# First rows of the first phase in a written order: ada_w ahead of x, three of eight row blocks on TensorE, the modulation on ScalarE

## The chip, the cores and the metric

One core of a Trainium2 chip runs the whole program in one launch. TensorE (PE) multiplies, VectorE (DVE), ScalarE (ACT) and GpSimd (POOL) do elementwise work, SyncE (SP) issues the large loads. The metric is the device time of one execution in microseconds (us), lower is better.

## The reference

Two layers of a decoder trunk on x of 256 tokens by 1024, in fp32. A layer has three sub-layers, each modulated by a conditioning vector c: a half-step SwiGLU (d_ff 2816), a token mixer (gated DeltaNet, MoBA attention and mLSTM heads side by side, one projection in, one out), and another SwiGLU. The change touches the head of the first sub-layer of layer 0:

```
mod = (silu(c) @ ada_w[l] + ada_b[l]).reshape(b, 3, 3, 1024)
h   = x * (1 + scale) + shift                  # mod[:, 0, 1], mod[:, 0, 0]
a, b = split(h @ w13, 2)                       # w13: 1024 x 5632
y   = (silu(a) * b) @ w2
x   = layer_norm(ALPHA*x + 0.5*(1 + gate)*y, ln_g, ln_b)
```

## The kernel before

An fp32 product is made of three products of rounded parts: `split` (lines 94 to 102) rounds a weight tile to `hi` on ScalarE (L98) and takes `lo` as the rest on VectorE (L100); `mm3` (L104 to L106) accumulates hi by xh, hi by xl and lo by xh in PSUM.

The first phase (layer 0, first SwiGLU) begins with `first_rows`. It computes the first seven of 22 column blocks of w13 while the modulation is still being made, k block by k block (the 1024 rows of w13 in eight blocks of 128). For each k, `modulate(k)` loads a piece of ada_w, `araw` (1024 rows by 128 shift and 128 scale columns, 1 MB in two DMAs), and a row block of w13, `raw` (two DMAs of 448 KB). VectorE sums the eight 128-row blocks of the piece, each times its column of silu(c), into `ada` (L594, L596); TensorE sums `ada` over its partitions with a matmul of one column (L598); VectorE adds the bias columns `abc` (L600, L601), ScalarE makes xh (L603), VectorE xm and xl (L605, L606). Then come 42 products of 256 columns: seven blocks f, two halves ab, three each. x itself is loaded first, in one DMA (L1299), and transposed into xT (L567). The seven PSUM banks (`pss`: four named pg, three pacc) are opened with a product by zero (L580).

`param_columns` (L186 to L195) transposes four groups of parameter rows into columns on TensorE (L183), with a copy on VectorE (L184): abc for both layers, lnc (layer norm), cvc (convolutions).

Behind the first rows, `ffn` handles the other column blocks in chunks of two, their raw tiles loaded 1 MB at a time (L82), with `sg` (silu, L631), `h` (L633), `hh` and `hl` (L638, L639) per block. In between stand background pieces for later modulations: `adacc` on VectorE (L253, L255), with their own 1 MB pieces of ada_w.

Except for SyncE, whose order is the program's, a scheduler decides the order of each engine's instructions from its own estimate, over the whole program. Buffers set the rest: `araw` has three, `raw` four, `hi` eight, `lo` four.

The mixer (one per layer) holds, for the steps below: `at` (L935, VectorE; a product of the DeltaNet heads with its decay), `MB` (L1175, VectorE, and L1176, ScalarE; mLSTM gate terms that arrive by a DMA through DRAM), and `U` (L1053, ScalarE; a copy of the DeltaNet heads' solved values out of PSUM).

## Time and profile before

| | us |
|---|---|
| median of 3 runs | 1238.44 (1237.76, 1238.44, 1243.74) |
| the profiled execution itself | 1244.06 |
| its span | 1242.3 |
| mean granted TensorE clock | 0.966 of full |

The profile shows one execution. Starts are us from the span's start. A row of a timeline gives start, duration, engine, line, operation, output and inputs, the number of instructions in the row, and in brackets the idle time ahead of it and what ended that. Rows with several instructions are runs without a gap; an instruction's duration overlaps the next one's start. TensorE's ends are modelled, so the distance from start to start is the better measure there. The granted clock is 1.00 at 2.4 GHz and 0.50 at 1.2 GHz. An fp32 matmul leaves two records.

### The profile page before, as it was taken

The numbers are of one execution on the slowest core, as the hardware profiler recorded it, in microseconds if no ns is written. First come the engines' busy times: TensorE is split into PE (matmuls) and PEld (weight loads), VectorE is DVE, ScalarE is ACT, GpSimd is POOL, SyncE is SP. The second block draws the span as 40 slices with busy tenths as digits, with TensorE's granted clock in tenths as the row PEclk, the third lists the DMA queues.
The fourth block names the chain that finished last, engine by engine and source line by source line (L and its number), as shares of the span: only waits on it lengthen the run. The fifth ranks groups of instructions, "written<-read, shape, count | busy, mean of one in ns | idle before, by whom it ended". The sixth has DMA issues, their size and how long they took to land.

```text
span 1242.3 us, 21704 instructions
## 1 busy us (share of the span) xinstructions
PE 1169.5 (94%) x8896; PEld 1075.6 (87%) x8896; DVE 899.2 (72%) x1451; ACT 577.9 (47%) x946; POOL 104.0 (8%) x174
## 2 busy tenths in 40 slices
...
GB/s 306 343 306 369 283 410 277 117 178 130 120 174 57 35 269 373 338 275 303 261 11 345 333 282 260 254 239 77 186 129 97 170 46 74 256 220 181 244 203 34
DMA packets 171523, 266.02 MB, mean 214 GB/s; under 512 B 5406, under 2 KB 136986, under 8 KB 171424
## 3 DMA queue, kind: packets, MB, share of 16 engines
...
q14 instruction: 30, 0.25, 0.1%
HBM read 263.56 MB, written 1.06 MB: 213 GB/s over the span
## 4 chain that ended last, share of the span: by engine, by line
PE 74%; DVE 9%; DMA 6%; ACT 5%; issue 3%; POOL 2%; SPq 0%; DVEq 0%; ACTq 0%; POOLq 0%
PE pg L105 14%; PE pg L106 14%; PE pg L104 14%; PE pacc L106 7%; PE pacc L105 7%; PE pacc L104 7%; DMA raw<-in_ffn_w_dram 4%; DVE lo L100 2%; ACT hi L98 2%; PE pg L220 1%; POOL xt L961 1%; DMA raw<-in_w_in_dram 1%; PE pg L228 1%; POOL X L963 1%; ACT xh L446 1%
## 5 line engine op out<-in xcount | busy, mean ns | idle before, releaser
L100 DVE TENSOR_TENSOR lo<-raw,hi 128x1024 fp32r<-128x1024 f32 (+3 forms) x332 | 395.1, 1196 | 146.7 <-PE pg L105 69.5
L98 ACT ACTIVATE hi<-raw 128x1024 fp32r<-128x1024 f32 (+4 forms) x352 | 352.3, 1027 | 305.7 <-DMA raw<-in_ffn_w_dram 144.6
L104 PE MATMUL pg<-xh,hi 128*128 128x256 f32 x1568 | 448.2, 288 | 5.7 <-ACT xh L603 2.9
L105 PE MATMUL pg<-xl,hi 128*128 128x256 f32 x1568 | 448.6, 286 | 1.5 <-DVE xl L606 1.5
L106 PE MATMUL pg<-xh,lo 128*128 128x256 f32 x1568 | 448.3, 286 | 0.2 <-DVE lo L100 0.2
L104 PEld LDWEIGHTS pg<-xh,hi 128*128 128x128 f32 x1568 | 302.8, 194 | 8.5 <-ACT xh L603 3.8
L105 PEld LDWEIGHTS pg<-xl,hi 128*128 128x128 f32 x1568 | 305.0, 194 | 3.2 <-DVE xl L606 2.0
L106 PEld LDWEIGHTS pg<-xh,lo 128*128 128x128 f32 x1568 | 304.7, 195 | 0.8 <-DVE lo L100 0.4
L255 DVE SCALAR_TENSOR_TENSOR adacc<-araw,sc__132,adacc 128x1024 f32<-128x1024 f32 x118 | 151.1, 1281 | 8.6 <-DMA araw<-in_ada_w_dram 8.0
L105 PE MATMUL pacc<-lo,hh 128*128 128x512 f32 (+1 forms) x352 | 128.9, 367 | 2.4 <-DVE lo L100 2.4
L104 PE MATMUL pacc<-hi,hh 128*128 128x512 f32 (+1 forms) x352 | 130.4, 371 | 0.0
L106 PE MATMUL pacc<-hi,hl 128*128 128x512 f32 (+1 forms) x352 | 129.6, 369 | 0.0
L172 POOL TENSOR_TENSOR lsm<-lsm,mhalf 128x1 f32<-128x1 f32 x12 | 7.5, 627 | 888.6 <-DVE lsm L344 888.6
L105 PEld LDWEIGHTS pacc<-lo,hh 128*128 128x128 f32 x352 | 66.5, 189 | 16.8 <-DVE lo L100 3.6
L104 PEld LDWEIGHTS pacc<-hi,hh 128*128 128x128 f32 x352 | 66.2, 188 | 12.8 <-issue 0.7
L106 PEld LDWEIGHTS pacc<-hi,hl 128*128 128x128 f32 x352 | 66.0, 188 | 11.8
L631 ACT ACTIVATE sg<-pg 128x256 f32<-128x256 f32 x79 | 29.4, 373 | 65.9 <-PE pg L106 65.8
L104 PE MATMUL pacc<-hi,xh 128*128 128x512 f32 (+1 forms) x80 | 38.1, 476 | 20.7 <-ACT xh L446 20.7
L638 ACT ACTIVATE hh<-h 128x256 fp32r<-128x256 f32 x82 | 33.7, 411 | 41.4 <-DVE h L633 41.3
L639 DVE TENSOR_TENSOR hl<-h,hh 128x256 fp32r<-128x256 f32 x82 | 34.5, 421 | 22.5 <-ACT hh L638 22.5
L722 DVE SCALAR_TENSOR_TENSOR cy<-pg,cvc,cy 128x255 f32<-128x255 f32 (+2 forms) x90 | 40.0, 474 | 7.0 <-ACT cy L720 6.7
L104 PEld LDWEIGHTS pacc<-hi,xh 128*128 128x128 f32 x80 | 19.3, 241 | 27.5 <-ACT xh L446 25.8
...
## 6 DMA issues: line engine op xcount, KB each, us to landing
...
```

Source lines behind the costliest of these rows:

```text
L98: nc.scalar.activation(hi, v, AF.Copy)
L100: nc.vector.tensor_tensor(lo, v, hi.bitcast(F32), op=ALU.subtract)
L104: nc.tensor.matmul(o, ah, bh, start=first, stop=False)
L105: nc.tensor.matmul(o, ah, bl, start=False, stop=False)
L106: nc.tensor.matmul(o, al, bh, start=False, stop=last)
L220: nc.tensor.matmul(pt[:, m:m + 1], acc[:, m * 128:(m + 1) * 128], ones[:, 0:1], start=True, stop=True)
L228: nc.tensor.matmul(pts[h], ones, acc[:, h * 512:(h + 1) * 512], start=True, stop=True)
L255: nc.vector.scalar_tensor_tensor(acc, raw[:, kk, :], sc_[:, k:k + 1], acc, op0=ALU.mult, op1=ALU.add)
L631: nc.scalar.activation(sg, pa, AF.Silu)
L638: nc.scalar.activation(hh[:, f, :], h, AF.Copy)
L639: nc.vector.tensor_sub(hl[:, f, :], h, hh[:, f, :].bitcast(F32))
L722: nc.vector.scalar_tensor_tensor(y[:, s:], ps[:, :T - s], w(3 - s), y[:, s:], op0=ALU.mult, op1=ALU.add)
```

## The change

`first_rows` is written anew, its instructions on TensorE, VectorE and ScalarE in the order of the code (`manual_schedule`), and not by the scheduler.

- Loads: the first ada_w piece goes ahead of x, x comes in two halves of 512 columns with the first w13 block in between, and the loads run two k ahead.
- Modulation: VectorE sums five of the eight row blocks. TensorE takes the other three from the raw piece, with a column of silu(c) as moving operand (L610), and adds VectorE's sum (L611): for each k, eight fp32 matmuls of one column where there were two.
- ScalarE makes xm as well as xh, and all four copies of xT.
- The last two PSUM banks serve for the transposes of x first and are opened later.
- `param_columns` transposes only the first group up front; the other three (`more_columns`) are issued behind the first rows.

The diff, with the code that comes in:

```diff
--- before.py
+++ after.py
@@ -191,8 +191,8 @@
             nc.scalar.dma_start(rows[48:96, 2, :], ln_b.rearrange("l s (k p) -> (l s k) p", p=128))
             nc.scalar.dma_start(rows[0:72, 3, :], gdn_conv.rearrange("l j (k p) -> (l j k) p", p=128))
             nc.scalar.dma_start(rows[72:120, 3, :], mlstm_conv.rearrange("l j (k p) -> (l j k) p", p=128))
-            for i, (n, dst) in enumerate(((72, abc[:, 0:72]), (72, abc[:, 72:144]), (96, lnc), (120, cvc))):
-                column(rows[:n, i, :], n, dst)
+            column(rows[:72, 0, :], 72, abc[:, 0:72])
+            return lambda: [column(rows[:n, i, :], n, dst) for i, n, dst in ((1, 72, abc[:, 72:144]), (2, 96, lnc), (3, 120, cvc))]
 
         rc = ap_.tile([KD, 128], F32, tag="gate", name="rc", bufs=2)
         nc.sync.dma_start(rc, c.rearrange("o (k p) -> (o k) p", p=128))
@@ -560,60 +560,120 @@
 
             xin = state["xa"]
             xT = ap_.tile([128, KD, T], F32, tag="n", name="xT")
-            for q in range(0, KD, 2):
-                pt = ps_g()
+            xh = ap_.tile([128, KD, T], F32R, tag="xh", name="xh")
+            xl = ap_.tile([128, KD, T], F32R, tag="xl", name="xl")
+            cps = ps_acc(1)
+            pss = [ps_g() for _ in range(4)] + [ps_acc(t) for t in (0, 0, 1)][:nf - 4]
+            raws, wrs, xms = {}, {}, {}
+
+            nv = 5
+
+            def load_mod(k):
+                raws[k] = fpool[0].tile([128, KD, 2, 128], F32, tag="araw", name="araw", bufs=3)
+                for j in range(2):
+                    o = j * D + k * 128
+                    nc.sync.dma_start(raws[k][:, :, j, :], ada_w[0, :, o:o + 128].rearrange("(k p) f -> p k f", p=128))
+
+            def load_w(k):
+                wrs[k] = wp.tile([128, 2, nf * 128], F32, tag="raw", name="raw", bufs=4)
+                for ab in range(2):
+                    nc.sync.dma_start(wrs[k][:, ab, :], w13[l, i, k * 128:(k + 1) * 128, ab * DFF:ab * DFF + nf * 128])
+
+            def load_x(q):
+                sl = slice(q * 512, (q + 1) * 512)
+                nc.sync.dma_start(xin[:, :, sl], x[0].rearrange("(t p) d -> p t d", p=128)[:, :, sl])
+
+            def turn(q):
+
+                pt = pss[(0, 1, nf - 2, nf - 1)[q // 2]]
                 for k in (q, q + 1):
                     for t in range(2):
                         nc.tensor.transpose(pt[:, (k - q) * 256 + t * 128:(k - q) * 256 + (t + 1) * 128],
                                             xin[:, t, k * 128:(k + 1) * 128], ident)
-                v = pt.rearrange("p (a b) -> p a b", a=2)
-                if q % 4:
-                    nc.vector.tensor_copy(xT[:, q:q + 2, :], v)
-                else:
-                    nc.scalar.activation(xT[:, q:q + 2, :], v, AF.Copy)
-            xh = ap_.tile([128, KD, T], F32R, tag="xh", name="xh")
-            xl = ap_.tile([128, KD, T], F32R, tag="xl", name="xl")
-            cps = ps_acc(1)
-            pss = [ps_g() for _ in range(4)] + [ps_acc(t) for t in (0, 0, 1)][:nf - 4]
-
-            for ps in pss:
+                nc.scalar.activation(xT[:, q:q + 2, :], pt.rearrange("p (a b) -> p a b", a=2), AF.Copy)
+
+            def open_(ps):
+
                 nc.tensor.matmul(ps, zero.to_broadcast([1, 128]), zero.to_broadcast([1, 512]), start=True, stop=False)
-            wrs = {}
 
             def modulate(k):
-                raw = fpool[0].tile([128, KD, 2, 128], F32, tag="araw", name="araw", bufs=3)
-                for j in range(2):
-                    o = j * D + k * 128
-                    nc.sync.dma_start(raw[:, :, j, :], ada_w[0, :, o:o + 128].rearrange("(k p) f -> p k f", p=128))
-                wrs[k] = wp.tile([128, 2, nf * 128], F32, tag="raw", name="raw", bufs=4)
-                for ab in range(2):
-                    nc.sync.dma_start(wrs[k][:, ab, :], w13[l, i, k * 128:(k + 1) * 128, ab * DFF:ab * DFF + nf * 128])
+                raw = raws[k]
                 a = fpool[0].tile([128, 2, 128], F32, tag="h", name="ada", bufs=2)
-                for kk in range(KD):
+                for kk in range(nv):
                     if kk == 0:
                         nc.vector.tensor_scalar(a, raw[:, kk], sc_[:, kk:kk + 1], None, op0=ALU.mult)
                     else:
                         nc.vector.scalar_tensor_tensor(a, raw[:, kk], sc_[:, kk:kk + 1], a, op0=ALU.mult, op1=ALU.add)
                 for j in range(2):
-                    nc.tensor.matmul(cps[:, 2 * k + j:2 * k + j + 1], a[:, j, :], ones[:, 0:1], start=True, stop=True)
+                    o = cps[:, 2 * k + j:2 * k + j + 1]
+                    for kk in range(nv, KD):
+                        nc.tensor.matmul(o, raw[:, kk, j, :], sc_[:, kk:kk + 1], start=kk == nv, stop=False)
+                    nc.tensor.matmul(o, a[:, j, :], ones[:, 0:1], start=False, stop=True)
+
+            def apply(k):
                 sh, sc1 = modc[0][:, k:k + 1], modc[0][:, 8 + k:9 + k]
-                nc.vector.tensor_add(sh, cps[:, 2 * k:2 * k + 1], abc[:, k:k + 1])
                 nc.vector.scalar_tensor_tensor(sc1, cps[:, 2 * k + 1:2 * k + 2], 1.0, abc[:, 8 + k:9 + k],
                                                op0=ALU.add, op1=ALU.add)
+                nc.vector.tensor_add(sh, cps[:, 2 * k:2 * k + 1], abc[:, k:k + 1])
                 nc.scalar.activation(xh[:, k, :], xT[:, k, :], AF.Identity, bias=sh, scale=sc1)
-                xm = fpool[0].tile([128, T], F32, tag="sg", name="xm", bufs=2)
-                nc.vector.tensor_scalar(xm, xT[:, k, :], sc1, sh, op0=ALU.mult, op1=ALU.add)
-                nc.vector.tensor_sub(xl[:, k, :], xm, xh[:, k, :].bitcast(F32))
-
-            modulate(0)
-            for k in range(KD):
-                if k + 1 < KD:
-                    modulate(k + 1)
+                xms[k] = fpool[0].tile([128, T], F32, tag="sg", name="xm", bufs=2)
+                nc.scalar.activation(xms[k], xT[:, k, :], AF.Identity, bias=sh, scale=sc1)
+
+            def high(k):
+                ws = []
                 for ab in range(2):
-                    hi, lo = split(wrs[k][:, ab:ab + 1, :])
-                    for f in range(nf):
-                        mm3(pss[f][:, ab * 256:(ab + 1) * 256], hi[:, 0, f * 128:(f + 1) * 128],
-                            lo[:, 0, f * 128:(f + 1) * 128], xh[:, k, :], xl[:, k, :], False, ab == 1 and k == KD - 1)
+                    hi = wp.tile([128, 1024], F32R, tag="hi", name="hi", bufs=8)[:, :nf * 128]
+                    nc.scalar.activation(hi, wrs[k][:, ab, :], AF.Copy)
+                    ws.append((hi, wp.tile([128, 1024], F32R, tag="lo", name="lo", bufs=4)[:, :nf * 128]))
+                return ws
+
+            def low(k, ab, w):
+                nc.vector.tensor_tensor(w[ab][1], wrs[k][:, ab, :], w[ab][0].bitcast(F32), op=ALU.subtract)
+
+            def low_x(k):
+                nc.vector.tensor_sub(xl[:, k, :], xms[k], xh[:, k, :].bitcast(F32))
+
+            def products(k, ab, w, f0=0, f1=nf):
+                hi, lo = w
+                for f in range(f0, f1):
+                    mm3(pss[f][:, ab * 256:(ab + 1) * 256], hi[:, f * 128:(f + 1) * 128],
+                        lo[:, f * 128:(f + 1) * 128], xh[:, k, :], xl[:, k, :], False, ab == 1 and k == KD - 1)
+            E = mybir.EngineType
+            with tc.manual_schedule(engines={E.PE, E.DVE, E.Activation}):
+                load_mod(0), load_x(0), load_w(0), load_x(1), load_mod(1), load_w(1)
+                turn(0), turn(2)
+                modulate(0)
+                apply(0)
+                ws = high(0)
+                low(0, 0, ws), low_x(0), low(0, 1, ws)
+                for ps in pss[:-2]:
+                    open_(ps)
+                for k in range(KD):
+                    if k + 2 < KD:
+                        load_mod(k + 2), load_w(k + 2)
+                    now = ws
+                    if k + 1 < KD:
+                        ws = high(k + 1)
+                    if k == 0:
+
+                        products(0, 0, now[0], 0, nf - 2)
+                        products(0, 1, now[1], 0, nf - 2)
+                        turn(4), turn(6)
+                    else:
+                        products(k, 0, now[0])
+                    if k + 1 < KD:
+                        modulate(k + 1)
+                        low(k + 1, 0, ws)
+                        apply(k + 1)
+                        low(k + 1, 1, ws), low_x(k + 1)
+                    if k == 0:
+                        for ps in pss[-2:]:
+                            open_(ps)
+                        products(0, 0, now[0], nf - 2)
+                        products(0, 1, now[1], nf - 2)
+                    else:
+                        products(k, 1, now[1])
+            more_columns()
             return xh, xl, pss
 
         def ffn(l, i, xh, xl, nx, first=None):
@@ -1295,10 +1355,8 @@
         fpool = [None]
         fstack = contextlib.ExitStack()
         fpool[0] = fstack.enter_context(tc.tile_pool(name="ff00", bufs=1, reuse_waits="tile"))
-        xin = ap_.tile([128, 2, D], F32, tag="xa", name="xin")
-        nc.sync.dma_start(xin, x[0].rearrange("(t p) d -> p t d", p=128))
-        state["xa"] = xin
-        param_columns()
+        xin = state["xa"] = ap_.tile([128, 2, D], F32, tag="xa", name="xin")
+        more_columns = param_columns()
         phases = [(l, s) for l in range(DEPTH) for s in range(3)]
         xh = xl = first = None
         for j, (l, s) in enumerate(phases):
```

The order of the instructions shows what became of it at three places. Names ending in numbers there are single tiles.

TensorE at the end of the first rows, before: the last products of the first rows (L104 to L106 into a pacc bank), and then the first of the chunks (into pg).

```order
L105 MATMUL pacc_195<-xl,hi 128x256
L106 MATMUL pacc_195<-xh,lo 128x256
L104 MATMUL pacc_196<-xh,hi 128x256
L105 MATMUL pacc_196<-xl,hi 128x256
L106 MATMUL pacc_196<-xh,lo 128x256
L104 MATMUL pg<-xh,hi 128x256
L105 MATMUL pg<-xl,hi 128x256
L106 MATMUL pg<-xh,lo 128x256
L104 MATMUL pg<-xh,hi 128x256
```

The same place after (ident and rows are the identity and the rows of parameters):

```order
L105 MATMUL pacc_161<-xl,hi 128x256
L106 MATMUL pacc_161<-xh,lo 128x256
L104 MATMUL pacc_162<-xh,hi 128x256
L105 MATMUL pacc_162<-xl,hi 128x256
L106 MATMUL pacc_162<-xh,lo 128x256
L183 MATMUL pg<-ident,rows 128x72
L183 MATMUL pg<-ident,rows 128x96
L183 MATMUL pg<-ident,rows 128x120
L104 MATMUL pg<-xh,hi 128x256
L105 MATMUL pg<-xl,hi 128x256
L106 MATMUL pg<-xh,lo 128x256
```

The three transposes of parameter rows (L183) that stood at the program's start now stand between the last product and the first chunk.

VectorE there, before, from the columns of k = 7 on (modc is the modulation column, xl the modulated x's low part, lo a weight's low part, h and hl the first blocks' results):

```order
L255 SCALAR_TENSOR_TENSOR adacc<-araw,sc__132,adacc 128x1024
L600 TENSOR_TENSOR modc_134<-pacc_189,abc 128x1
L601 SCALAR_TENSOR_TENSOR modc_134<-pacc_189,abc 128x1
L255 SCALAR_TENSOR_TENSOR adacc<-araw,sc__132,adacc 128x1024
L605 TENSOR_SCALAR xm<-xT,modc_134 128x256
L100 TENSOR_TENSOR lo<-raw,hi 128x1024
L606 TENSOR_TENSOR xl<-xm,xh 128x256
L100 TENSOR_TENSOR lo<-raw,hi 128x1024 x2
L633 TENSOR_TENSOR h<-sg,pg 128x256
L255 SCALAR_TENSOR_TENSOR adacc<-araw,sc__132,adacc 128x1024
L633 TENSOR_TENSOR h<-sg,pg 128x256
L639 TENSOR_TENSOR hl<-h,hh 128x256
```

Three lo of chunk weights stand ahead of the first h. After, from the ada operations of k = 7 on:

```order
L606 SCALAR_TENSOR_TENSOR ada<-araw,sc__132,ada 128x256
L255 SCALAR_TENSOR_TENSOR adacc<-araw,sc__132,adacc 128x1024
L606 SCALAR_TENSOR_TENSOR ada<-araw,sc__132,ada 128x256
L631 TENSOR_TENSOR lo<-raw,hi 128x896
L615 SCALAR_TENSOR_TENSOR modc_134<-pacc_155,abc 128x1
L617 TENSOR_TENSOR modc_134<-pacc_155,abc 128x1
L631 TENSOR_TENSOR lo<-raw,hi 128x896
L100 TENSOR_TENSOR lo<-raw,hi 128x1024
L634 TENSOR_TENSOR xl<-xm,xh 128x256
L100 TENSOR_TENSOR lo<-raw,hi 128x1024 x3
L693 TENSOR_TENSOR h<-sg,pg 128x256 x2
L255 SCALAR_TENSOR_TENSOR adacc<-araw,sc__132,adacc 128x1024
```

The rows that follow at once, still VectorE after (abc, lnc and cvc are the parameter columns):

```order
L184 COPY abc<-pg 128x72
L699 TENSOR_TENSOR hl<-h,hh 128x256
L184 COPY lnc<-pg 128x96
L699 TENSOR_TENSOR hl<-h,hh 128x256
L255 SCALAR_TENSOR_TENSOR adacc<-araw,sc__132,adacc 128x1024
```

Two adacc operations stand between the ada operations of k = 7, a fourth lo stands ahead of the first h, and the copies of the parameter columns (L184) stand among the first blocks' results, the first behind an adacc.

VectorE in layer 1's mixer, before (at, MB as above; lo for the weights of the next projection; mem and mM of the mLSTM heads):

```order
L935 TENSOR_TENSOR at<-pgdn,dec 128x3x64
L1163 TENSOR_TENSOR mem<-mF,pm 128x12
L100 TENSOR_TENSOR lo<-raw,hi 128x768
L1175 SCALAR_TENSOR_TENSOR MB<-MB,mgs,mk 128x128 x6
L935 TENSOR_TENSOR at<-pgdn,dec 128x3x64 x2
L1175 SCALAR_TENSOR_TENSOR MB<-MB,mgs,mk 128x128 x2
L935 TENSOR_TENSOR at<-pgdn,dec 128x3x64
L1175 SCALAR_TENSOR_TENSOR MB<-MB,mgs,mk 128x128
L100 TENSOR_TENSOR lo<-raw,hi 128x768
L1175 SCALAR_TENSOR_TENSOR MB<-MB,mgs,mk 128x128 x2
L100 TENSOR_TENSOR lo<-raw,hi 128x768
```

The last two lo stand behind nine and eleven MB operations. After (L995 and L1235 are the former L935 and L1175, L1037 the former L977):

```order
L995 TENSOR_TENSOR at<-pgdn,dec 128x3x64
L1223 TENSOR_TENSOR mem<-mF,pm 128x12
L100 TENSOR_TENSOR lo<-raw,hi 128x768
L995 TENSOR_TENSOR at<-pgdn,dec 128x3x64 x3
L100 TENSOR_TENSOR lo<-raw,hi 128x768 x2
L1235 SCALAR_TENSOR_TENSOR MB<-MB,mgs,mk 128x128
L1037 TENSOR_TENSOR vv<-pgdn,brk__9131 128x384
L1235 SCALAR_TENSOR_TENSOR MB<-MB,mgs,mk 128x128 x4
L100 TENSOR_TENSOR lo<-raw,hi 128x768
L1235 SCALAR_TENSOR_TENSOR MB<-MB,mgs,mk 128x128
```

All four `at` and three lo now stand ahead of the first MB; before, six MB operations stood ahead of the last three `at`.

## Rows read from the trace of the kernel before

**Rows 1.** The page, parts 1 and 4: busy time by engine; the chain that ended last

```profile
PE 1169.5 (94%) x8896; PEld 1075.6 (87%) x8896; DVE 899.2 (72%) x1451; ACT 577.9 (47%) x946; POOL 104.0 (8%) x174
...
PE 74%; DVE 9%; DMA 6%; ACT 5%; issue 3%; POOL 2%; SPq 0%; DVEq 0%; ACTq 0%; POOLq 0%
```

**Rows 2.** Windows of the first phase: length; busy PE, PEld, DVE, ACT, POOL; clock; DMA; GB/s

```profile
19.47:69.00 49.53, 44.35 (x308) 43.48 (x309) 43.70 (x98) 20.61 (x25) 0.00 (x0) 0.84 1.04 321
69.00:236.00 167.00, 164.83 (x1160) 152.50 (x1159) 142.49 (x178) 71.68 (x110) 0.55 (x1) 1.00 0.88 320
```

**Rows 3.** Windows again, two stretches at half clock

```profile
18.20:28.40 10.20, 8.62 (x37) 7.74 (x37) 9.92 (x22) 3.96 (x5) 0.00 (x0) 0.50 1.15 328
59.20:62.50 3.30, 3.30 (x18) 3.30 (x17) 3.19 (x9) 2.11 (x3) 0.00 (x0) 0.50 1.04 392
```

**Rows 4.** Timeline of SP: start, duration, instruction [idle before <-what ended it]

```profile
1.26 0.41 SPq L1299 DMA_DIRECT2D xin<-in_x_dram  x1
1.72 1.08 SPq L587 DMA_DIRECT2D araw<-in_ada_w_dram  x2
```

**Rows 5.** Timeline of DVE at both ends of the first rows

```profile
10.88 0.35 DVE L594 TENSOR_SCALAR ada<-araw,sc__132 128x256 f32<-128x256 f32 x1 [4.33 <-DMA araw<-in_ada_w_dram]
...
11.67 0.25 DVE L184 COPY lnc<-pg 128x96 f32<-128x96 f32 x1
11.84 1.52 DVE L596 SCALAR_TENSOR_TENSOR ada<-araw,sc__132,ada 128x256 f32<-128x256 f32 x3
...
73.44 1.22 DVE L100 TENSOR_TENSOR lo<-raw,hi 128x1024 fp32r<-128x1024 f32 x1 [1.30 <-PE pacc L106]
75.67 0.42 DVE L633 TENSOR_TENSOR h<-sg,pg 128x256 f32<-128x256 f32 x1 [1.01 <-ACT sg L631]
76.01 1.28 DVE L255 SCALAR_TENSOR_TENSOR adacc<-araw,sc__132,adacc 128x1024 f32<-128x1024 f32 x1
```

**Rows 6.** Timeline of PE: transposes of x, first product with xl, a wait, the end

```profile
11.30 2.77 PE L567 MATMUL pg<-ident,xin 128*128 128x128 f32 x12
...
22.23 0.58 PE L105 MATMUL pg<-xl,hi 128*128 128x256 f32 x1 [0.89 <-DVE xl L606]
...
57.99 0.61 PE L598 MATMUL pacc<-ones,ada 128*128 128x1 f32 x4 [1.43 <-DVE modc L601]
...
75.52 0.28 PE L105 MATMUL pacc<-xl,hi 128*128 128x256 f32 x1
75.64 0.28 PE L106 MATMUL pacc<-xh,lo 128*128 128x256 f32 x1
76.15 0.39 PE L104 MATMUL pg<-xh,hi 128*128 128x256 f32 x1 [0.23 <-DVE h L633]
```

**Rows 7.** Timeline of PE, a group of one-column fp32 matmuls

```profile
135.54 1.84 PE L220 MATMUL pg<-ones,adacc 128*128 128x1 f32 x16
137.25 0.36 PE L104 MATMUL pg<-xh,hi 128*128 128x256 f32 x1
```

**Rows 8.** Timeline of ACT, last loads of the first rows and first of the chunks

```profile
55.81 0.95 ACT L98 ACTIVATE hi<-raw 128x896 fp32r<-128x896 f32 x1 [0.21 <-DMA raw<-in_ffn_w_dram]
57.97 0.60 ACT L603 ACTIVATE xh<-xT,modc 128x256 fp32r<-128x256 f32 x1 [1.21 <-DVE modc L601]
...
65.38 1.06 ACT L98 ACTIVATE hi<-raw 128x1024 fp32r<-128x1024 f32 x1 [1.44 <-PE pacc L105]
```

**Rows 9.** The mixers of layer 0 and layer 1, then the stall in layer 1

```profile
308.24:403.06 94.82, 92.41 (x1038) 83.55 (x1036) 60.52 (x141) 48.51 (x106) 29.21 (x52) 0.98 0.35 115
912.94:1015.10 102.16, 96.25 (x1038) 86.41 (x1036) 60.92 (x141) 48.52 (x105) 29.19 (x52) 0.95 0.33 107
970.00:975.00 5.00, 3.06 (x48) 2.48 (x47) 1.81 (x2) 3.65 (x9) 1.01 (x2) 0.89 0.68 210
```

**Rows 10.** Timeline of DVE, layer-1 mixer

```profile
957.18 2.55 DVE L1175 SCALAR_TENSOR_TENSOR MB<-MB,mgs,mk 128x128 f32<-128x128 f32 x6 [1.21 <-DMA MB<-nmd]
```

**Rows 11.** Timeline of ACT, layer-1 mixer

```profile
971.53 0.47 ACT L1053 ACTIVATE U<-pgdn 128x384 f32<-128x384 f32 x1
```

## The prediction

> **What bounds the kernel now.** I read the page first: which engine is busiest and which one the chain that ended last runs through. TensorE is busy for 94% of the span and carries 74% of the chain [rows 1], so an early saving counts only if TensorE itself moves on sooner. The table of stretches comes next: between 19.47 and 69 us TensorE works 44.35 of 49.53 us at a mean granted clock of 0.84 while the DMA share is full, and from 69 to 236 us it works 164.83 of 167 us [rows 2]. The reader is to see two things. The first rows are a mixed stage, with loads, VectorE and TensorE all close to full. Behind them there is no slack on TensorE, so a shift in the moment when the first chunk starts is carried, microsecond for microsecond, to the end of the phase. That moment is 76.15 us; the last product of the first rows started 0.51 us earlier [rows 6].
>
> The clock in the first rows comes from two half-clock stretches that I show, one of 10.2 us after the slow start and one of 3.3 us after a wait [rows 3], in which TensorE had idled 1.43 us ahead of one small group at 57.99 us [rows 6]. At full clock a product starts every 0.12 us (75.52 to 75.64) [rows 6], and half of a stretch at a granted clock of 0.50 is lost: about 1.7 us of 3.3, and 5.1 of 10.2.
>
> **The change, part by part.**
>
> *Loads.* Before, x (1 MB) is issued at 1.26 us and the first ada_w piece (1 MB) behind it [rows 4]; VectorE gets the piece at 10.88 us [rows 5]. That is 2 MB in 9.6 us; by share the piece alone would be there 4.8 us after issue, about 6.1, and half of x about 8.5. Both are estimates. The extra issue (x in two halves) costs some 0.4 us of SP's own time, hidden by the loads under way. The bytes stay, so the last w13 piece still lands near 55.8, where ScalarE takes it up [rows 8].
>
> *First product.* Five VectorE operations instead of eight, three of which take 1.52 us [rows 5], end near 8.6 us. Eight transposes of x at 0.23 us (twelve take 2.77 [rows 6]) end near 10.4, and with them the longer way starts: the one-column group 1.7 (below), two column operations 0.15, xh and xm 0.6 each, the first of two conversions 0.95 [rows 8], one subtraction about 1.0 (1.22 for the larger tile [rows 5]) and xl, taken like h, 0.34. That is 15.8 us; with 0.1 for each of eight hand-overs between engines (an estimate) the first product with xl starts near 16.6, against 22.23 [rows 6]. ScalarE's added xm (0.6 us for each k) lies beside the products: it works 20.61 us of 49.53 [rows 2].
>
> *One-column matmuls.* TensorE gets, for each of eight k, eight fp32 matmuls of one column where it had two. The same kind of group stands later: 16 records from 135.54, next product 137.25, so 1.7 us [rows 7]. Seven of these stand after the first product: 11.9 us. They are on the path: each stands in TensorE's queue between two runs of products. The 336 products take 336 x 0.12 = 40.3 us. Start at half clock as before: 5.1 us lost. End of the first rows: 16.6 + 40.3 + 11.9 + 5.1 = 73.9 us against 75.76, some 2 us earlier; 68.8 if the clock is full at once, about 76 if another stretch of 3.4 us at half clock falls in.
> The Trainium skill (FP8 and Floating Point Precision, section TensorE Precision Notes) gives true fp32 four passes through the array. The trace has two records for each such matmul, and by a reading of four records of 0.107 us each (an estimate from that page and the row) the seven groups would take 23.8 instead of 11.9 us. The time between the two rows contains whatever passes there are, so 1.7 stands.
>
> *k = 7.* In VectorE's new order two operations of 1.2 us for a later modulation (adacc) stand between the ada operations of k = 7. Their piece is the third transfer of 1 MB behind the last of w13, which ScalarE took up at 55.81 [rows 8]: 9.8 us at 321 GB/s [rows 2], so 65.6 at the latest; I take 64. TensorE wants the result of k = 7 at 73.9 - 5.0 (42 products) - 1.7 - 2.5 (21 products) = 64.7 us. It gets it at 64 + 1.2 + 0.4 + 1.2 = 66.8, or two later by the upper bound and by ScalarE, where the xh of k = 7 now stands behind five conversions of chunk data (the fourth in before stood at 65.38 [rows 8]). I add 2.0 us: the last product starts near 75.9, as before. Bounds 0 and 4.
>
> *End of the first rows.* The three column transposes left out at the start now stand in TensorE's queue between the last product and the first chunk. The third needs the copy of the first out of its bank, and the chunk's first product needs the second copy. On VectorE ahead of that copy stand: a lo that needs a buffer of the last products (it took 1.22 us), two h at 0.34 (from start to start), an adacc (1.28), a copy 0.17, hl, taken like h, and a copy 0.17 [rows 5]. With each about 0.08 shorter to the next start, and 0.1 for the hand-over, that is 1.14 + 0.68 + 1.20 + 0.17 + 0.34 + 0.17 + 0.1 = 3.8 us of idle TensorE, where before had 0.23 [rows 6]. So +3.6, and behind such a hole a stretch at half clock, +1.7. Cover could exist only if VectorE ran ahead, but its first operation there waits for TensorE itself. Bounds: 1.5 (the lo finds its buffer early) and 5.3.
> Whether the three transposes break the hole into short ones is a question to the clock. In before, the small group at 57.99, with the wait ahead of it, did not keep the clock up [rows 3, 6], so I take the 1.7. The Trainium skill (TensorE: Matmul & The Clock Gate, section Part 4: PE-mode transpose) says that a transpose does not count as a busy array in the way a product does; by it the 1.7 us are due, and without it the term would be 3.6 alone.
>
> First phase: 0 + 3.6 + 1.7 = +5.3 us, range -2 to +9.
>
> *Layer 1's mixer.* Nothing there is edited, but the scheduler places VectorE's, ScalarE's and TensorE's work anew. In before, layer 1's mixer takes 102.16 us where layer 0's takes 94.82 [rows 9]. Six MB operations stand on VectorE ahead of `at`; their data arrive by a DMA only at 957.18 [rows 10], everything behind them is late, ScalarE copies U at 971.53 [rows 11], and TensorE works 3.06 of the 5 us from 970, at a mean granted clock of 0.89 [rows 9]. After the change all four `at` and three lo stand ahead of any MB, and U ahead of the softmax. That could take back as much as 7.3 us (layer 0's pace) or nothing (the DMA is now issued behind two Y copies, so MB itself lands later and could stall VectorE in another place, +1.5). I take -5.
>
> **Sum.** +5.3 - 5 = +0.3 against the profiled execution's own 1244.06 us (span 1242.3). That execution lies 5.6 us above the median of the three timed runs, 1238.44, so part of its stall may be missing from them; for that doubt I add 0.3 to the +0.3. Predicted: 1238.44 + 0.6, 1239 us.
>
> **The rivals.**
> 1. *The early start reaches the end (faster).* If the half-clock stretch at the start is short and the adacc's data come early, the first rows end at 70 to 72 us, 4 to 6 us sooner; minus the 3.6 to 5.3 at their end the first phase is at -2 to +1, and the mixer brings -5 to -7.3. Together -4 to -9: 1229.5 to 1234.5. For it: TensorE's own sum without the clock's loss, 68.8. Against it: the same transposes and zero-opens with gaps stood ahead of the half-clock stretch in before.
> 2. *The transposes in TensorE's queue decide (slower).* One mechanism: between the last product of the first rows and the first chunk, TensorE waits for VectorE. Price 3.6 + 1.7, with the k = 7 wait at its upper bound 7.3; it decides as soon as the mixer brings less than 1 us, for instance since the timed runs had not its stall. +5.3 to +7.3: 1243.7 to 1245.7. For it: 167 us of TensorE without slack behind it [rows 2]. Against: the order in the mixer, where the release of `at` from MB is plain to see.
> 3. *One-column groups pull the clock down (slower).* 1.7 us of each 6.7 us per k are fed with one column. If a half-clock stretch followed three of them, +5.1 in all, the end would be 1244; all seven, 1251. Against: the clock stayed full after 135.54 in before, with the stretch from 69 to 236 us at 1.00 [rows 2, 7].
> 4. *It does nothing.* The loads set the first rows: the last piece at 55.8, then 20 us of work whatever the start. Then only the end and the mixer differ, which is again about 0, so it shares the forecast's time, 1239.
>
> **How the numbers follow.** About 0.5% (6.2 us) is what a measurement of this kernel can tell from no change. Forecast with rival 4: 0.54, own range 1234 to 1244. Rival 1: 0.24, of which most lies beyond -6.2. Rival 2: 0.15, half of it beyond +6.2. Rival 3: 0.07, nearly all beyond. Adding the tails of the forecast: faster 0.24, same 0.56, slower 0.20. The range that leaves out 2 in 10 runs from 1230 to 1247.
>
> **What would show each step.** First product with xl near 16.6 us. Sixteen records before each k's second half, 1.7 us, clock 1.00 around them from the third k on. End of the first rows near 76, and a wait on VectorE of more than 3 us ahead of the first chunk's product, with three transposes in it: if the chunk starts before 76, the largest term is wrong. A half-clock stretch right after it. In layer 1's mixer, `at` on VectorE ahead of MB, U copied some 5 us sooner after the mixer's start, its length near 97 us; if it stays at 102, rival 2 has won.

## The result and the profile after

The changed kernel takes 1248.88 us (median of 20 runs, 1240.07 to 1256.78), the kernel before 1239.17 (20 runs, 1230.90 to 1246.15): ratio 1.0065, 95% interval 1.0040 to 1.0089. By the ratio it is slower by some 8 us, where no change (1239) was forecast and 1247 was the upper end of the range. A second measurement (e7 below) gives 1.0038 (1.0015 to 1.0061).

The profiled execution of the changed kernel took 1240.88 us, the second lowest of its runs, less than the 1244.06 us of the one before. Read as a whole, the two profiles have the wrong sign; they have to be read stage by stage. The first stage is the first rows. TensorE in the changed kernel (start, duration, instruction, idle time ahead and what ended it):

```profile
9.25 1.97 PE L591 MATMUL pg<-ident,xin 128*128 128x128 f32 x8 [6.29 <-DMA xin<-in_x_dram]
11.01 1.28 PE L610 MATMUL pacc<-sc__132,araw 128*128 128x1 f32 x6
...
18.23 0.58 PE L105 MATMUL pg<-xl,hi 128*128 128x256 f32 x1 [0.88 <-DVE xl L634]
...
23.34 1.03 PE L591 MATMUL pacc<-ident,xin 128*128 128x128 f32 x8
...
30.57 0.73 PE L610 MATMUL pacc<-sc__132,araw 128*128 128x1 f32 x6
...
32.27 0.36 PE L104 MATMUL pg<-xh,hi 128*128 128x256 f32 x1
...
37.38 0.73 PE L610 MATMUL pacc<-sc__132,araw 128*128 128x1 f32 x6
...
67.27 0.38 PE L611 MATMUL pacc<-ones,ada 128*128 128x1 f32 x2 [1.87 <-DVE ada L606]
...
77.41 0.28 PE L106 MATMUL pacc<-xh,lo 128*128 128x256 f32 x1
79.34 0.72 PE L183 MATMUL pg<-ident,rows 72*128 72x72 f32 x2 [1.65 <-DVE h L693]
81.01 0.46 PE L183 MATMUL pg<-ident,rows 120*128 120x120 f32 x1 [0.95 <-DVE abc L184]
81.51 0.58 PE L104 MATMUL pg<-xh,hi 128*128 128x256 f32 x1
```

The first product with xl starts 4.0 us sooner than in [rows 6]. A one-column group takes 1.70 us (30.57 to 32.27), one k 6.81 us (30.57 to 37.38), without idle time. `ada` of k = 7 keeps TensorE waiting for 1.87 us. The last product nevertheless starts 1.8 us later than before's, and between it and the first chunk (81.51) stand the three transposes in a hole of 4.1 us: the first chunk starts 5.4 us later. The hole has two waits of about equal weight: 1.65 us for an h, ahead of the first transposes, and then the transposes with the wait for the copies of their results. What VectorE did there:

```profile
63.94 1.28 DVE L255 SCALAR_TENSOR_TENSOR adacc<-araw,sc__132,adacc 128x1024 f32<-128x1024 f32 x1 [1.09 <-DMA araw<-in_ada_w_dram]
65.14 0.47 DVE L606 SCALAR_TENSOR_TENSOR ada<-araw,sc__132,ada 128x256 f32<-128x256 f32 x1
65.54 1.28 DVE L255 SCALAR_TENSOR_TENSOR adacc<-araw,sc__132,adacc 128x1024 f32<-128x1024 f32 x1
...
77.73 1.23 DVE L100 TENSOR_TENSOR lo<-raw,hi 128x1024 fp32r<-128x1024 f32 x1 [1.29 <-PE pacc L106]
78.87 0.75 DVE L693 TENSOR_TENSOR h<-sg,pg 128x256 f32<-128x256 f32 x2
79.53 1.28 DVE L255 SCALAR_TENSOR_TENSOR adacc<-araw,sc__132,adacc 128x1024 f32<-128x1024 f32 x1
80.73 0.23 DVE L184 COPY abc<-pg 128x72 f32<-128x72 f32 x1
...
81.20 0.25 DVE L184 COPY lnc<-pg 128x96 f32<-128x96 f32 x1
```

The adacc operations hold up k = 7, and the copy that releases the first chunk's bank (81.20) stands behind lo, two h, an adacc, a copy and an hl. The same stretches as windows (length; busy PE, PEld, DVE, ACT, POOL; granted clock; DMA share; GB/s):

```profile
18.23:69.00 50.77, 48.90 (x399) 48.37 (x400) 35.98 (x72) 24.36 (x34) 0.00 (x0) 1.00 1.01 314
81.51:239.60 158.09, 156.82 (x1079) 145.09 (x1079) 131.97 (x160) 64.96 (x94) 0.56 (x1) 0.98 0.86 315
79.70:86.50 6.80, 5.81 (x25) 5.29 (x26) 6.80 (x13) 2.16 (x8) 0.00 (x0) 0.50 1.05 352
```

Against [rows 2], TensorE is the full engine of the first rows now, busy for 48.90 of 50.77 us at a granted clock of 1.00 (up to 21.6 us products still start every 0.21 us and not every 0.12; the clock is on record only from 21.7), and VectorE has room. Behind the hole come 6.8 us at half clock. The next boundary (first transposes behind the first phase, L434 before) comes at 239.6 us against 232.0.

The second stage is layer 1's mixer, from its second scores (where the first `at` is made) to the transposes of the next boundary. First the window of the kernel before:

```profile
952.80:1030.10 77.30, 72.32 (x592) 60.54 (x589) 51.80 (x121) 36.83 (x81) 12.35 (x16) 0.96 0.36 119
```

Then the changed kernel's, and its copy of U:

```profile
948.90:1027.60 78.70, 72.36 (x595) 60.28 (x591) 51.24 (x121) 36.66 (x81) 13.75 (x16) 0.96 0.37 126
```

```profile
961.13 0.47 ACT L1113 ACTIVATE U<-pgdn 128x384 f32<-128x384 f32 x1
```

And the waits of TensorE in the two windows by what ended them (us in total, times, longest), before and then changed:

```profile
PE pacc L105 <- DVE lo L100: 2.9, 4, 1.3
PE pgdn L1061 <- ACT U L1053: 1.9, 1, 1.9
...
PE pacc L105 <- DVE lo L100: 2.9, 4, 1.3
PE pg L1252 <- DVE mP L1249: 1.4, 2, 1.2
PE pmb L1319 <- ACT bP L1306: 1.1, 1, 1.1
PE pgdn L296 <- DVE mix L1284: 0.5, 1, 0.5
PE pm L1325 <- ACT bPT L1321: 0.4, 1, 0.4
```

The first three of these new waits in the changed kernel's timeline:

```profile
978.29 0.55 PE L1319 MATMUL pmb<-ident,bP 128*128 128x128 f32 x3 [1.06 <-ACT bP L1306]
986.51 0.43 PE L1325 MATMUL pm<-vb,bPT 128*128 128x64 f32 x2 [0.43 <-ACT bPT L1321]
989.30 0.44 PE L1252 MATMUL pg<-vc,mP 128*128 128x65 f32 x2 [1.15 <-DVE mP L1249]
```

U is copied 12.2 us after the second scores, against 18.7 before (971.53 - 952.8, [rows 11]), and yet the stretch is 1.4 us longer: the 1.9 us of waiting for U are gone, but 3.5 us came in the tail, for the softmax rows (bP and their transposed copy bPT), for the mLSTM's mP and for mix, which stand behind. The 2.9 us for lo are in both. Both windows hold one half-clock stretch of 6.8 us (973.9 to 980.7 before, behind the wait for U; 991.1 to 997.9 changed, behind the wait for mP). The whole mixer, over the window of [rows 9], takes 100.2 us instead of 102.2, not 97: 1.7 of these 2.0 us are a half-clock stretch of 3.4 us that only before has, ahead of its second scores (932.97 to 936.38).

### The profile page after: what moved, and what is told of

Same layout as the page of the kernel before. It is cut to its first block, busy times and chain, and to the rows that moved or that the text cites. A ratio compares the mean times of both kernels' runs of the same rounds, so it can differ in the third digit from the quotient of the medians.

```text
span 1239.2 us, 21859 instructions
## 1 busy us (share of the span) xinstructions
PE 1168.0 (94%) x8992; PEld 1076.7 (87%) x8992; DVE 887.1 (72%) x1417; ACT 583.9 (47%) x956; POOL 104.9 (8%) x174
## 4 chain that ended last, share of the span: by engine, by line
PE 74%; DVE 9%; ACT 6%; DMA 5%; issue 3%; POOL 2%; SPq 0%; DVEq 0%; ACTq 0%; POOLq 0%
PE pg L104 14%; PE pg L106 14%; PE pg L105 14%; PE pacc L106 7%; PE pacc L105 7%; PE pacc L104 7%; ACT hi L98 2%; DVE lo L100 2%; PE pg L220 1%; DMA raw<-in_ffn_w_dram 1%; POOL xt L1021 1%; DMA raw<-in_w_in_dram 1%; POOL X L1023 1%; PE pg L228 1%; DVE xl L451 1%
## 5 line engine op out<-in xcount | busy, mean ns | idle before, releaser
L100 DVE TENSOR_TENSOR lo<-raw,hi 128x1024 fp32r<-128x1024 f32 (+3 forms) x316 | 378.2, 1203 | 157.4 <-PE pg L105 69.6
L98 ACT ACTIVATE hi<-raw 128x1024 fp32r<-128x1024 f32 (+2 forms) x336 | 337.5, 1031 | 281.6 <-DMA raw<-in_ffn_w_dram 91.0
L104 PE MATMUL pg<-xh,hi 128*128 128x256 f32 x1568 | 450.4, 287 | 2.9 <-DVE cy L782 1.5
L106 PE MATMUL pg<-xh,lo 128*128 128x256 f32 x1568 | 447.3, 286 | 0.1
L104 PEld LDWEIGHTS pg<-xh,hi 128*128 128x128 f32 x1568 | 303.9, 194 | 5.5 <-ACT hi L98 2.1
L106 PEld LDWEIGHTS pg<-xh,lo 128*128 128x128 f32 x1568 | 303.5, 194 | 0.8 <-DVE lo L100 0.4
L104 PE MATMUL pacc<-hi,hh 128*128 128x512 f32 (+1 forms) x352 | 130.3, 371 | 0.0
L106 PE MATMUL pacc<-hi,hl 128*128 128x512 f32 (+1 forms) x352 | 129.6, 369 | 0.0
L105 PEld LDWEIGHTS pacc<-lo,hh 128*128 128x128 f32 x352 | 66.5, 189 | 15.9 <-DVE lo L100 2.9
L104 PEld LDWEIGHTS pacc<-hi,hh 128*128 128x128 f32 x352 | 66.2, 188 | 12.6 <-issue 0.7
L106 PEld LDWEIGHTS pacc<-hi,hl 128*128 128x128 f32 x352 | 66.0, 188 | 11.8
L104 PE MATMUL pacc<-hi,xh 128*128 128x512 f32 (+1 forms) x80 | 35.0, 437 | 20.6 <-ACT xh L446 20.6
L104 PEld LDWEIGHTS pacc<-hi,xh 128*128 128x128 f32 x80 | 17.0, 212 | 27.0 <-ACT xh L446 25.7
```

Of the source, the lines that this page charges most:

```text
L98: nc.scalar.activation(hi, v, AF.Copy)
L100: nc.vector.tensor_tensor(lo, v, hi.bitcast(F32), op=ALU.subtract)
L104: nc.tensor.matmul(o, ah, bh, start=first, stop=False)
L105: nc.tensor.matmul(o, ah, bl, start=False, stop=False)
L106: nc.tensor.matmul(o, al, bh, start=False, stop=last)
```

## The experiments

Measured is the ratio to runs of the kernel before on the same chip, with its interval; 0.1% is 1.24 us. Line numbers in a variant may be one or two off.

**e1: columns up front again.**

```diff
-            column(rows[:72, 0, :], 72, abc[:, 0:72])
-            return lambda: [column(...) for i, n, dst in (...)]
+            for i, (n, dst) in enumerate(((72, abc[:, 0:72]), ..., (120, cvc))):
+                column(rows[:n, i, :], n, dst)
+            return lambda: None
```

> The changed kernel with all four groups of parameter columns transposed up front again, as in before. Theory (the three transposes between the first rows and the first chunk hold TensorE for 4.1 us, 77.41 to 81.51, and 6.8 us at half clock follow): the hole shrinks to about 0.3 us, the first chunk starts near 77.5 us, no half-clock stretch right behind it, and the median comes back to before's within 3 us (ratio 0.998 to 1.002). Rival A (the one-column matmuls on TensorE are the price): the hole goes but the time stays at least 5 us above before, ratio 1.004 to 1.007. Rival B (the rearranged order of later phases is the price): likewise above before, with the loss behind 240 us.

Measured: 1241.02 us, 0.9989 (0.9966 to 1.0012). The time came back as the theory has it, but not where it says. The hole shrinks to 1.9 us and not to 0.3, since TensorE waits for an h there without any transposes:

```profile
81.95 0.39 PE L104 MATMUL pg<-xh,hi 128*128 128x256 f32 x1 [1.65 <-DVE h L694]
```

So the late transposes make some 2.2 of the 4.1 us. And the first chunk starts no sooner, because the first product waits 2.5 us longer (20.8) and the last comes at 80.0. The boundary is at 236.9, 2.7 us sooner than changed, as no half-clock stretch follows the shorter hole. The rest lies behind it: the two mixers take 73.5 and 70.4 us from their second scores, 6 us less together.

**e2: all eight row blocks on VectorE.**

```diff
-            nv = 5
+            nv = 8
...
-                    nc.tensor.matmul(o, a[:, j, :], ones[:, 0:1], start=False, stop=True)
+                    nc.tensor.matmul(o, a[:, j, :], ones[:, 0:1], start=nv == KD, stop=True)
```

> The changed kernel with VectorE summing all eight row blocks of ada_w again, TensorE none (two one-column matmuls for each k, as before); loads, written order, ScalarE's share and late columns stay. Theory (late columns are the price): VectorE has 1.2 us more for each k and TensorE 1.0 us less; the last product comes 0 to 4 us sooner than 77.41, but the hole of about 4 us and the half-clock stretch stay; median 3 to 8 us above before (1.002 to 1.0065). Rival A (one-column matmuls are the price): about 8 us less than the changed kernel, at or below before, ratio 0.998 to 1.000.

Measured: 1257.74 us, 1.0128 (1.0096 to 1.0161). Rival A is not borne out: without the one-column matmuls the kernel is slower still, and by more than forecast. But that is no clean test of their price, since the version has a loss of its own: first chunk 85.6 (the xl of k = 6 stands on VectorE behind an adacc that waits 6.3 us for its data, and TensorE waits 6.7 us for it), layer 0's mixer 79.5.

**e3: both undone**, by the edits of e1 and e2.

> Both undone: columns up front, eight row blocks on VectorE. Left are the loads, the written order and ScalarE's share; TensorE's and ScalarE's order behind the first rows is then the same as before's, instruction for instruction. Theory: first chunk between 72 and 76 us, so 0 to 4 us sooner than before's 76.15, ratio 0.997 to 1.000. Rival C (the first rows are set by loads, the last w13 piece near 55.8 and 20 us of work behind it, whatever the start): first chunk at 76 and ratio 1.000. Rival B: since later order equals before's, ratio 1.000 with either of e1 and e2 well above.

Measured: 1245.74 us, 1.0026 (1.0001 to 1.0051). Behind the first rows TensorE and ScalarE have before's order, and the mixers take what they take in before (71.4 and 77.7). The written order itself is not sooner: first chunk at 81.6, where 72 to 76 was expected. The trace shows why, in two of TensorE's waits:

```profile
56.89 0.61 PE L612 MATMUL pacc<-ones,ada 128*128 128x1 f32 x4 [0.89 <-DVE ada L607]
66.17 0.58 PE L105 MATMUL pg<-xl,hi 128*128 128x256 f32 x1 [5.93 <-DVE xl L635]
```

With eight operations for each k VectorE sets a pace of 6.6 to 6.7 us (the wait of 0.89 us stands at 43.6, 50.3 and 56.9). The 5.93 us are for the xl of k = 6, and VectorE shows what is ahead of it:

```profile
64.49 1.28 DVE L256 SCALAR_TENSOR_TENSOR adacc<-araw,sc__132,adacc 128x1024 f32<-128x1024 f32 x1 [5.52 <-DMA araw<-in_ada_w_dram]
65.69 0.42 DVE L635 TENSOR_TENSOR xl<-xm,xh 128x256 fp32r<-128x256 f32 x1
```

The scheduler put an adacc there whose data had not landed, and the earlier start is lost to it.

**e4: late columns alone**, in the kernel before.

```diff
...
+            more_columns()
             return xh, xl, pss
```

> The kernel before with one thing moved: the last three groups of parameter columns are transposed behind the first rows, as in the changed kernel; all else as before (the scheduler orders the first rows). Theory: a hole of 2 to 4 us ahead of the first chunk (it starts near 79 us against 76.15) and a half-clock stretch behind it, median 3 to 7 us above before (1.0025 to 1.0055). Rival A or B: no change (0.999 to 1.001), since the transposes then find TensorE waiting for the loads or are placed elsewhere by the scheduler.

Measured: 1254.78 us, 1.0101 (1.0067 to 1.0135). The hole is there (columns: as above):

```profile
76.22 0.31 PE L183 MATMUL pg<-ident,rows 72*128 72x72 f32 x2
79.36 0.32 PE L183 MATMUL pg<-ident,rows 120*128 120x120 f32 x1 [2.83 <-DVE abc L184]
79.53 0.39 PE L104 MATMUL pg<-xh,hi 128*128 128x256 f32 x1
```

It shifts the first chunk by 3.4 us and the boundary by 4.9, as the theory has it; a half-clock stretch of 3.4 us follows (80.90 to 84.31). The other half was expected by nobody: layer 0's mixer went from 71.4 to 77.4 us, since the scheduler ordered it differently.

**e5 and e6: columns elsewhere.** e5 calls `more_columns()` behind the second pair of column blocks. e6 puts them behind the products of k = 1, into spare columns of the modulation's bank:

```diff
...
+                    if k == 1:
+                        more_columns(cps)
```

> The changed kernel with the three late column transposes issued still later, behind the second pair of column blocks of the first phase, where TensorE has products queued ahead of them. Theory (the place between the first rows and the first chunk is the price, not the lateness): the first chunk starts near 77.8 us (1.6 above before), no hole above 0.5 us, no half-clock stretch from 79 to 87, and the median is 6 to 9 us below the changed kernel's, ratio to before 0.998 to 1.002. Rival A (one-column matmuls are the price): ratio stays at 1.004 to 1.008.

> The changed kernel with the three transposes inside the written order, behind the products of k = 1, into spare columns of the bank that holds the modulation sums. They cost TensorE about 0.4 us there and VectorE three copies of 0.2 us. Theory: first chunk near 78 us, no hole, ratio to before 0.998 to 1.002, equal to the version with the columns behind the second pair within 3 us. Rival A: 1.004 to 1.008. If both are below 0.998, the early start is worth more than the one-column matmuls cost.

Measured: e5 1242.93 us, 1.0000 (0.9977 to 1.0023); e6 1238.82, 0.9974 (0.9948 to 1.0000). By their medians they lie 5 and 9 us below the changed kernel on the same chip (e7). e6 has no hole; in e5 the 1.65 us for h stay, as in e1. But the first chunk moves little (81.6 and 80.2), since the last product comes 2.3 to 2.7 us later and 6.8 us at half clock lie around 70 us, where the changed kernel's two profiles have 3.4 and none. More comes from layer 1's mixer: 74.1 and 70.4 us.

**e7: the changed kernel again.**

> The changed kernel itself, for a second profile: the first one (1240.88 us) lies 8 us below its median of 1248.88. Theory: the first phase is the same to within 1 us (first chunk at 81.5, boundary near 239.6), and the time above 1241 is found as further half-clock stretches behind 240 us; mean granted clock near 0.973, ratio 1.004 to 1.009. Rival: the first phase itself varies by several us from run to run.

Measured: 1248.05 us, 1.0038 (1.0015 to 1.0061); its profiled execution has a span of 1250.2 us. The first phase is the same to 1.3 us (first chunk 81.2, boundary 238.3). The two profiles differ by 11 us of span, and behind the first phase by their half clock: 45 us at 0.50 in the first, 76 in the second, stretches such as the one below. Half of the 31 us is 15; part of it falls into waits.

```profile
247.90:265.00 17.10, 15.64 (x63) 15.22 (x62) 4.61 (x12) 5.06 (x10) 0.00 (x0) 0.50 0.00 1
```

**e8: x ahead of ada_w.**

```diff
-                load_mod(0), load_x(0), load_w(0), load_x(1), load_mod(1), load_w(1)
+                load_x(0), load_x(1), load_mod(0), load_w(0), load_mod(1), load_w(1)
```

> The changed kernel with both halves of x loaded ahead of the first ada_w piece, as before had it; all else as changed. Theory (the first rows are set by TensorE's own queue from the first product on): the first product with xl starts 2 to 4 us later than 18.23, the last product as much later, and the median is 1 to 4 us above the changed kernel, ratio 1.007 to 1.010. Rival C (loads set the end of the first rows, the early start is hidden): last product and time as in the changed kernel, ratio 1.0065 within 2 us.

Measured: 1254.65 us, 1.0097 (1.0066 to 1.0127). First product at 19.8, first chunk at 83.5, both 1.6 to 2.0 later. The first rows do follow their first product; but the boundary is at 239.4, as in the changed kernel, since behind a hole of the same 4.1 us with the same three transposes no half-clock stretch came here (79.75 to 86.57 in the changed kernel). The rest is the mixers, 78.2 and 78.8 us.

**e9 and e10: one constraint on the mixers**, in before and in the changed kernel:

```diff
...
+                        with tc.issue_after(state["los"][-2].ins):
                             nc.vector.scalar_tensor_tensor(w, w, gs[:, t, h:h + 1], mk, op0=ALU.add, op1=ALU.min)
```

> The kernel before with one constraint in the mixers: VectorE's MB operations stand behind the last but one lo of the mixer's projections, so behind all `at` and three lo in layer 1. Theory (the MB operations ahead of `at` and lo are what makes layer 1's mixer slow): from its second scores to the next boundary layer 1 takes 70 to 74 us instead of 77.3, and the median falls by 3 to 7 us, ratio 0.9945 to 0.998. Rival (as in the changed kernel, where `at` stands ahead of MB and U is copied 6.5 us sooner, the gain is lost again in the mixer's tail): 76 us or more there, ratio 0.999 to 1.001.

> The changed kernel with the same constraint, which gives layer 1's mixer the same order on VectorE as in e9. Theory: the mixers then cost the same in both, and what is left between this kernel and e9 is the first phase, 6 to 8 us (0.5 to 0.65%); against before the ratio is 1.000 to 1.003. Rival (first phase is not the price): within 2 us of e9.

Measured: e9 1242.27 us, 0.9993 (0.9966 to 1.0020); e10 1246.22, 1.0040 (1.0018 to 1.0063). In e9 layer 1's stretch falls to 72.1 us, but layer 0's rises to 73.3, and the sum is too small for the interval: inconclusive. Between e9 and e10 lie 4 us, with 6.3 between their boundaries.

**e11: row blocks on TensorE alone**, in the kernel before.

```diff
-                for kk in range(KD):
+                for kk in range(5):
...
+                    for kk in range(5, KD):
+                        nc.tensor.matmul(o, raw[:, kk, j, :], sc_[:, kk:kk + 1], start=kk == 5, stop=False)
```

> The kernel before with one part of the change alone: TensorE multiplies three of the eight row blocks of ada_w (eight one-column matmuls for each k), VectorE five; loads, columns, scheduler's order of the first rows as before. Its layer-1 mixer has the same order as the changed kernel's. Theory: 78.6 us there against before's 77.3, so +1.3, as in the changed kernel; in the first rows VectorE has 1.2 us less for each k, TensorE 1.1 more: first chunk between 74 and 79 us; ratio 0.999 to 1.004. Rival A (one-column matmuls are the price): first chunk beyond 81, ratio above 1.005.

Measured: 1239.57 us, 0.9978 (0.9945 to 1.0010), no loss in all. But the first phase is longer by 3.6 us (first chunk 79.7 behind a wait of 2.15 us for h, boundary 235.6), although TensorE ran from 24.1 to 77.3 us without a wait and without the later half-clock stretch that before has there [rows 3]; only the mixers make up for it. So the one-column matmuls do have a price in the first rows. Layer 1's mixer, in nearly the changed kernel's order, took 73.6 us here and not 78.7, without a half-clock stretch in it.

**e12: e6 with k = 7 freed**, the first adacc operations held behind the last xl.

```diff
...
+                        with tc.issue_after(state["xl"].ins) if (l, blk) == (0, 2) else after_ln("dve") if k == 0 else contextlib.nullcontext():
```

> The version with the columns in k = 1, and VectorE's first adacc operations held back until the last xl of the first rows, so that they don't stand between the ada operations of k = 7. Both mixers get the order that layer 1's had there. Theory: TensorE's wait of 1.8 us for k = 7 and the half-clock stretch of 6.8 us behind it go, the first chunk starts at 75 to 77.5 us against 80.2, the mixers take about 71 us each from their second scores, and the median is 5 to 9 us below before, ratio 0.9925 to 0.996. Rival C (loads set the end of the first rows): first chunk still near 80, ratio 0.996 to 0.998.

Measured: 1235.46 us, 0.9939 (0.9906 to 0.9973): faster than both kernels, by 0.6% than before. Not for the reason given: the first chunk stays at 80.3. TensorE's wait only changed hands, to an xh behind a conversion that waits for its data:

```profile
72.80 0.38 PE L104 MATMUL pg<-xh,hi 128*128 128x256 f32 x1 [1.89 <-ACT xh L618]
```

```profile
71.20 1.06 ACT L98 ACTIVATE hi<-raw 128x1024 fp32r<-128x1024 f32 x1 [2.86 <-DMA raw<-in_ffn_w_dram]
```

Both mixers, however, are short (windows from the second scores, layer 0 and layer 1), 7.8 us less than before's together:

```profile
353.20:423.70 70.50, 67.46 (x585) 56.84 (x582) 51.72 (x121) 36.60 (x81) 12.63 (x16) 1.00 0.31 102
954.80:1025.20 70.40, 67.36 (x583) 56.77 (x580) 51.44 (x121) 36.21 (x80) 12.53 (x16) 1.00 0.40 131
```

**e13: layer 1's mixer alone**, the constraint of e9 with [-3]; first rows and layer 0 as before.

> The kernel before with the MB operations of VectorE held behind one lo further on; first rows and layer 0 keep before's order, layer 1's mixer alone changes (`at` and two lo ahead of MB, U still behind the four softmax rows). Theory (the mixer's order alone is worth several us): from its second scores to the next boundary 71 to 74 us instead of 77.3, and the median 3 to 6 us below before, ratio 0.995 to 0.998, first phase unchanged. Rival: 76 us or more, or a shorter mixer with no change of the median (0.999 to 1.001), the gain lost to the clock elsewhere.

Measured: 1236.36 us, 0.9965 (0.9935 to 0.9995). The boundary is at 231.8, layer 0's stretch 71.4, and layer 1's:

```profile
954.30:1027.10 72.80, 69.77 (x592) 58.48 (x590) 51.75 (x121) 36.85 (x81) 13.75 (x16) 1.00 0.39 127
```

4.5 us less in the mixer, 4.3 less in the time: the order of that mixer alone moves the kernel. Gone are the wait for U (1.9 us) and the half-clock stretch behind it (half of 6.8 us).

**e14 and e15: e12 with ScalarE's conversions held as well**, e15 with `nv = 6`.

> The version e12 with ScalarE's conversions for the second pair of column blocks held behind the xm of k = 7 as well (one of them waited for its data ahead of the last xh). Its layer-1 mixer falls into the changed kernel's order. Theory: first chunk at 77 to 78.5 us against e12's 80.3, so 2 to 3 us gained, and 5 to 8 us lost again in layer 1's mixer (75 to 79 us against 70.4): median 2 to 6 us above e12's, ratio to before 0.995 to 0.999. Rival (mixer order without weight): 2 to 3 us below e12, ratio 0.991 to 0.993.

> The same with six row blocks on VectorE and two on TensorE (six one-column matmuls for each k). Both mixers get one of the short orders. Theory (TensorE's queue sets the pace of the first rows, 6.8 us for each k with 1.7 of one-column work): 0.4 us less for each k, first chunk at 74.5 to 76.5, mixers 70 to 72 us each, median 8 to 11 us below before, ratio 0.991 to 0.9935. Rival C (loads at 6.0 us for each k, the last w13 piece, set the end): first chunk as in e14.

Measured: e14 1235.71 us, 0.9970 (0.9944 to 0.9996); e15 1237.03, 0.9969 (0.9938 to 1.0000). The first rows behave as expected, first chunk 78.7 and 75.2 (before 76.15), so TensorE's queue does set their pace: 16 one-column matmuls fewer, of 0.21 us each, are 3.4 us, and 3.5 were measured. e14's layer-1 mixer took 73.5 us, where 75 to 79 was expected. e15 stays 5 us above what its stages give, and above its expected 0.991 to 0.9935: a stretch between the scores of layer 0 was 5 us longer, with 10.2 us at half clock in it, where before has 3.4.

**All of them together.** From one profile each: the boundary behind the first phase, and the two mixers from second scores to the next boundary; as differences from before (232.0; 71.4 + 77.3 us), their sum, and what the ratio gives on 1240 us. The last two columns are explained below the table.

| | boundary | mixers | sum | measured | without the clock | by the clock |
|---|---|---|---|---|---|---|
| changed | +7.6 | +1.3 | +8.9 | +8.1 | | |
| changed again (e7) | +6.3 | +1.3 | +7.6 | +4.7 | +8.5 | -3.9 |
| e1 | +4.9 | -4.8 | +0.1 | -1.4 | +8.4 | -9.9 |
| e2 | +10.8 | +2.2 | +13.0 | +15.9 | +10.0 | +5.6 |
| e3 | +4.5 | +0.4 | +4.9 | +3.2 | +8.1 | -4.6 |
| e4 | +4.9 | +6.1 | +11.0 | +12.5 | +2.2 | +10.3 |
| e5 | +7.2 | -3.2 | +4.0 | 0.0 | +6.8 | -6.5 |
| e6 | +4.0 | -6.9 | -2.9 | -3.2 | +4.1 | -7.5 |
| e8 | +7.4 | +8.3 | +15.7 | +12.0 | +13.8 | -2.2 |
| e9 | +1.6 | -3.3 | -1.7 | -0.9 | 0.0 | -0.3 |
| e10 | +7.9 | +1.5 | +9.4 | +5.0 | +9.7 | -5.6 |
| e11 | +3.6 | -3.8 | -0.2 | -2.7 | +5.7 | -7.6 |
| e12 | +4.0 | -7.8 | -3.8 | -7.6 | +3.4 | -10.0 |
| e13 | -0.2 | -4.6 | -4.8 | -4.3 | +0.3 | -4.1 |
| e14 | +1.6 | -4.7 | -3.1 | -3.7 | +4.0 | -8.4 |
| e15 | -1.9 | -6.9 | -8.8 | -3.8 | +0.3 | -3.9 |

These stretches, a first phase and two mixers, account for each to within 5 us, over a range of 24. The windows were chosen afterwards, and a profile can lie up to 8 us from its kernel's median. The mixers of 70.4 us hold fewer records of TensorE (583 in e12, 592 before): nine products stand ahead of the second scores there, some 1 us.

The clock of these runs is on record too, and it changes the reading. The last two columns take the mean granted clock's shortfall times the span as what the clock cost a run (an estimate; the first 15 to 28 us of the profiles carry no record of it) and divide the difference of the mean times from before on the same chip into the rest and the clock's part, with standard errors of some 1 us and 1 to 2.5. So the changed kernel lost more than its time says, and before runs at a lower mean clock than it does (0.971 against 0.974). By this estimate e1 came back by the clock alone, e13 gains nearly all by it, and the one-column matmuls alone (e11) add some 6 us that the clock hides.

## Why the prediction was wrong, step by step

- **First product**: 16.6 forecast, 18.23 measured. The one-column group of k = 0 ran at the slow pace of the start, from 11.01 to 14.36, 3.3 us instead of 1.7. Behind it the start at half clock was cheaper than the 5.1 us forecast: products started slowly only up to 21.6, which cost 1.7 (half of 3.4 us).
- **One-column groups**: 1.70 us each, 6.8 us for each k, as forecast; TensorE full. Left out of the sum were the eight later transposes of x and the two late bank openings, 0.9 and 0.5 us on the same queue.
- **k = 7**: the adacc's data at 63.9 (64 forecast), a wait of 1.87 us (2.0). Right. But 3.4 us at half clock followed (69.51 to 72.92), 1.7 us that the sum lacked. Last product 77.4 instead of 75.9: +1.6, +1.4 and +1.7 by these points, -3.4 by the start.
- **End of the first rows**: hole 4.1 us, 3.8 forecast. Right, and e4 shows it alone; though by e1 and e5 a wait of 1.65 us for h stands there without the transposes too. The clock behind it, forecast at 1.7 us, cost 3.4 in this profile (6.8 us at 0.50), 1.7 in that of e7 (3.4 us) and nothing in e8. The Trainium skill's rule that a transpose does not count as a busy array in the way a product does (TensorE: Matmul & The Clock Gate, Part 4: PE-mode transpose) is not decided by this: the same three transposes in a hole as long were followed by 6.8, 3.4 and 0 us at half clock.
- **First phase**: +5.3 forecast, +7.6 and +6.3 in the two profiles, inside its range.
- **Layer 1's mixer**: this is the step that failed. "I take -5" was read from the order, and the order did what it says: U was copied 6.5 us sooner after the scores. But of the 5.0 us that TensorE was idle in before's stretch only the 1.9 for U went, and the new order, which has U ahead of the softmax, made the softmax, mP and mix late: 3.5 us of new waits, 6.3 us of idle TensorE in all, and the same 6.8 us at half clock. The window grew by 1.4 us; the whole mixer took 2.0 us less, not 5, and 1.7 of these by the clock. I had priced the removal of a wait and nothing for what the same move put last. That layer 1's mixer can be 4 to 7 us shorter is true: e13, e6 and e12, with U behind the first softmax rows, and e11 and e14, with U ahead of them. None of the five has a half-clock stretch in it, and that alone is 3.4 us.
- **The sum**: +5.3 - 5 = 0 became +6.3 to +7.6 and +1.3 (-2.0 over the whole mixer), so +4 to +9, where the two measurements give +4.7 and +8.1. Rival 2, the transposes with no gain in the mixer (1243.7 to 1245.7, chance 0.15), comes nearest, but 1248.88 lies above it, and of its mechanism only part is shown: the transposes made about half of the hole. The price of the one-column matmuls was in the forecast's sum (11.9 us), and e11, e14 and e15 bear it out. Rival 3 is out: the clock stayed at 1.00 between 21.7 and 69.5 us with seven of the groups in it.

That the last product comes 2 us later in e5 and e6 than in the changed kernel with the same start is mostly the clock: with half of the half-clock stretches taken off, first to last product take 57.5 us (changed), 57.9 (e7), 58.2 (e5) and 58.4 (e6, with the three transposes in it). Open is what decides whether and for how long the clock falls behind a wait. Nearly the same order of layer 1 took 78.7 us twice (changed, e7) and 73.5 twice (e11, e14). In the former two ScalarE makes one bPT copy of the tail two bP later; they have 2.1 us more of waits (for bPT, mP and mix) and 6.8 us at half clock, which begin 1.8 to 1.9 us behind the wait for mP and make 3.4. Together these are the 5 us, but that the one copy brings on both was not tested alone.
